# The output projection's first tile moves into attention's last steps, and two residual tiles are loaded with it

## The chip, the cores and the metric

The kernel runs on one core of one Trainium2 chip. Its time is the device time of one execution in microseconds (us), and lower is better. The profile's engines are PE (TensorE: matmuls and transposes), PEld (its weight loads), DVE (VectorE), ACT (ScalarE), POOL (GpSimd) and SP (SyncE, which issues most DMAs).

## What is computed

Two layers over 1024 frames of width 1024: one with a recurrent mixer, one with chunked attention, each with a squared-ReLU MLP behind it. The change is in the second layer, between attention's last head and the end of the output projection:

```python
def chunk_attention(hn, w_q, q_norm_g, rel_bias, w_o, k_pad, v_pad):
    ...
    out = lax.map(one_chunk, (q_chunks, jnp.arange(n_chunks)))     # 16 heads of 64
    out = out.transpose(1, 0, 2, 3, 4).reshape(bsz, s, d)
    return out @ w_o
...
h = h + g1[:, None, :] * y                                         # y: what attention returns
hn = modulate(rms_norm(h, norm2_g[layer]), sh2, sc2)
h = h + g2[:, None, :] * sqrelu_mlp(hn, mlp_w1[layer], mlp_w2[layer])
```

## The kernel before

Activations lie transposed: a tile of h, of attention's output or of a product has 128 features on the partitions and 1024 frames along the free dimension, so each is a list of 8 tiles. A product is made in halves of 512 frames, one PSUM bank each. For accuracy every operand is split into a high part and the remainder, and `mm3` makes three matmuls of each product (high by high, high by low, low by high: L329, L330, L331).

**Attention** goes in 64 steps, `todo`: 16 heads `hd`, four steps `j` each, 256 queries a step. Iteration `n` of the loop issues `scores` of step `n`, `trans` of step `n - 3` and `values` of step `n - 4`. `scores` writes a score tile of two PSUM banks (pool `ps2`, two such tiles), and DVE (L1569), ACT (L1571) and POOL (L1576) make softmax weights of it in SBUF. `trans` transposes these on PE (L1601) into up to three banks of pool `pa` (four banks), and `split` copies each to SBUF as high part (ACT, L334) and remainder (DVE, L335). `values` multiplies by V (L1620, L1621) into one more bank of `pa` for two steps together; behind an odd `j`, ACT (L1628) and DVE (L1629) read it out. Behind the last step of an odd head, POOL makes of the pair of heads the operand of the output projection, `oh[p]` (L1633) and `ol[p]` (L1635). There are eight pairs, the last behind step 63.

**The output projection** comes behind the loop. The pools of attention are closed, and a new pool `pz` takes all eight banks. The eight tiles of h are loaded back from DRAM (`hsp`) on ACT's queue (L1668). For each of eight tiles `m` of the result and each half, `proj` makes 8 x 3 = 24 matmuls, one `mm3` for each pair `k`, and DVE evicts the bank by multiplying by the gate and adding h (L1674). `n4_.sq` then stores the tile half to DRAM from SP's queue (L599) and squares it on ACT for the next norm. The last four tiles run in `tail`, with the norm between.

**Weights** come through `ws`, a stream: SP loads a tile (L159), ACT and DVE split it (L196, L200), and `ws.next()` hands it out in order: eight tiles of `w_o`, then the MLP's `w1`. Two steps before the end of attention `ws.hold` is lifted, and the stream loads and splits the first tiles of `w_o` beside the last head.

**What sets the order.** Up to L1162 the order is written by hand; from there the Tile framework's scheduler places each instruction on its engine's queue when the program is built, and within a queue each engine goes in that order. Dependencies go by tiles: the first user of a tile waits for the last user of what lay there before.

Of the kernel before, what the change touches and what calls it, by code (L numbers as in the profile page):

```python
# [8 lines left out]
F32 = mybir.dt.float32  # L9
F32R = mybir.dt.float32r  # L10
AF = mybir.ActivationFunctionType
ALU = mybir.AluOpType
# [4 lines left out]
KD = 8  # L17
# [286 lines left out]
def trunk(ctx: ExitStack, tc: tile.TileContext, I, out, dbg=None, stop=None):  # L304
    nc = tc.nc
    V, A_, PE, G = nc.vector, nc.scalar, nc.tensor, nc.gpsimd
# [6 lines left out]
    pools = {"b": pp.__enter__()}  # L313
    dp = ctx.enter_context(tc.tile_pool(name="dp", bufs=1, space=bass.MemoryType.DRAM))
    cnt = [0]

    def slot(dt=F32, tag="a", shape=(128, 1024)):
        cnt[0] += 1
        return ap_.tile(list(shape), dt, name=f"s{cnt[0]}", tag=tag)

    def bank(shape=(128, 512)):
        cnt[0] += 1
        return pools["b"].tile(list(shape), F32, name=f"b{cnt[0]}", tag="b")

    def hs(half):
        return slice(half * HALF, (half + 1) * HALF)

    def mm3(ps, ah, al, bh, bl, start, stop, more=False):
        PE.matmul(ps, ah, bh, start=start, stop=False, skip_group_check=more)  # L329
        PE.matmul(ps, ah, bl, start=False, stop=False, skip_group_check=more)  # L330
        return PE.matmul(ps, al, bh, start=False, stop=stop, skip_group_check=more).ins  # L331
# [19 lines left out]
    mods = [cp.tile([128, 48], F32, name=f"mod{l}") for l in range(2)]  # L351
    kvmod = cp.tile([128, 16], F32, name="kvmod")
    aa = cp.tile([128, 40], F32, name="aa")


    ws = Stream(nc, slot, whp, wsp)
# [291 lines left out]
    def proj(it, half, hh, hl):  # L648

        ps = bank()  # L650
        for k in range(KD):
            c = slice(k * 128, (k + 1) * 128)
            mm3(ps, it["hi"][:, c], it["lo"][:, c], hh[k][:, hs(half)], hl[k][:, hs(half)],
                k == 0, k == KD - 1)
        return ps
# [420 lines left out]
    h = []  # L1076
# [56 lines left out]
    for j in range(4):  # L1133
        for e in range(2):
            chunk(j, 1, e)
            n = 2 * j + e
# [16 lines left out]
    def mlp(l, h, nrm, nxt, last=None):  # L1153
        with ExitStack() as given:
            if l:
                given.enter_context(tc.manual_schedule())
            ws.timed = ws.early = True
            h = mlp_body(l, h, nrm, nxt, last)
            ws.drain()
            ws.timed = ws.early = False  # L1160
        if l == 0:
            order.close()  # L1162
        return h
# [210 lines left out]
    h = mlp(0, h, n2, n3)  # L1374
# [5 lines left out]
    hsp = dp.tile([KD, 128, S], F32, name="hsp")  # L1380
# [45 lines left out]
    for g in range(2):  # L1426
# [7 lines left out]
        out=gqk, in0=gqk, scalar=-(HD ** -0.5), in1=gk, op0=ALU.mult, op1=ALU.mult))  # L1434
# [40 lines left out]
    for n in range(2):  # L1475
        x1, x2, x3 = slot(F32R), slot(F32R), slot(F32R)

        def view(t):
            return t.rearrange("p (n q) -> p n q", n=4)


        hi = [view(x1)[:, 0:2], view(x1)[:, 2:4], view(x2)[:, 0:2]]
        lo = [view(x3)[:, 0:2], view(x3)[:, 2:4], view(x2)[:, 2:4]]
# [59 lines left out]
    def widths(i):  # L1543
        return 128 * min(3, max(0, i - 1))

    def scores(hd, j):
        R = prep[hd]
        bn = bns[hd % 2]
        ptile = []
        sm = cp.tile([128, 8], F32, name=f"sm{hd}_{j}", tag="sm", bufs=4)  # L1550
        for e in range(2):
            i = 2 * j + e
            w = widths(i)
            ql = R["q"][:, i * 128 : (i + 1) * 128]
            cnt[0] += 1
            sc = pools["s"].tile([128, 1024], F32, name=f"sc{cnt[0]}", tag="s")
            if w:
                k0 = (i - 1) * 128 - w
                PE.matmul(sc[:, 512 - w : 512], ql, R["k"][:, k0 : k0 + w], start=True, stop=False)
                PE.matmul(sc[:, 512 - w : 512], ql, R["kl"][:, k0 : k0 + w], start=False, stop=True)  # L1560
            c0 = 128 if i == 0 else 0
            k0 = max(0, (i - 1) * 128)
            k1 = (i + 1) * 128
            PE.matmul(sc[:, 512 + c0 : 768], ql, R["k"][:, k0:k1], start=True, stop=False)
            PE.matmul(sc[:, 512 + c0 : 768], ql, R["kl"][:, k0:k1], start=False, stop=True)
            m, s1 = sm[:, e : e + 1], sm[:, 2 + e : 3 + e]
            lo = 384 + c0 - w
            p = slot()
            V.tensor_tensor_reduce(out=p[:, lo:640], in0=sc[:, lo + 128 : 768], in1=bn[:, lo:640],  # L1569
                                   op0=ALU.add, op1=ALU.min, scale=1.0, scalar=BIG, accum_out=m)  # L1570
            A_.activation(out=p[:, lo:640], in_=p[:, lo:640], func=AF.Exp, scale=-1.0, bias=m,  # L1571
                          accum_out=s1)
            ptile.append((p, lo))
        V.reciprocal(out=sm[:, 4:6], in_=sm[:, 2:4])  # L1574
        for e, (p, lo) in enumerate(ptile):
            G.tensor_scalar(out=p[:, lo:640], in0=p[:, lo:640], scalar1=sm[:, 4 + e : 5 + e],  # L1576
                            scalar2=1.0, op0=ALU.mult, op1=ALU.mult)
        ptile = [p for p, lo in ptile]
        return ptile
# [3 lines left out]
    oh, ol = [None] * 8, [None] * 8  # L1583
# [58 lines left out]
    N = len(todo)  # L1642
    LAG = 3
    for n in range(N + LAG + 1):
        if n < N:
            hd, j = todo[n]
            if j >= 1 and hd + 1 < NH:
                prepare(hd + 1, j - 1)
            if j == 2 and hd == NH - 1:
                ws.hold = None  # L1650
                ws.pump()
            ptl[n] = scores(hd, j)
        if 0 <= n - LAG < N:
            trans(*todo[n - LAG], ptl.pop(n - LAG), n - LAG)
        if 0 <= n - LAG - 1 < N:
            values(*todo[n - LAG - 1], n - LAG - 1)
# [2 lines left out]
        return  # L1659


    ps2.__exit__(None, None, None)
    pp.__exit__(None, None, None)
    pp = ctx.enter_context(tc.tile_pool(name="pz", bufs=8, space=bass.MemoryType.PSUM))
    pools["b"] = pp
    h = [slot() for _ in range(KD)]
    for k in range(KD):
        nc.scalar.dma_start(h[k], hsp[k])  # L1668
    n4_ = NormS(h, aa[:, 24:32], mods[1][:, 24:32])
    g1b = mods[1][:, 16:24]  # L1670

    def oproj(m, it, half):
        ps = proj(it, half, oh, ol)
        V.scalar_tensor_tensor(out=h[m][:, hs(half)], in0=ps, scalar=g1b[:, m : m + 1],  # L1674
                               in1=h[m][:, hs(half)], op0=ALU.mult, op1=ALU.add)
        return [m]

    for m in range(4):
        it = ws.next()
        for half in range(2):  # L1680
            oproj(m, it, half)
            n4_.sq(m, hs(half))
        ws.done(it)
    its = [ws.next() for _ in range(4)]
    tail(its, lambda n, it, half: oproj(4 + n, it, half), n4_)
    dump("h3", h)

# [107 lines left out]
```

## Time and profile before

| | us |
|---|---|
| median of 3 runs | 2350.58 (2346.15 to 2351.51) |
| the profiled execution, its own time | 2348.78 |
| its span in the trace | 2346.9 |
| TensorE busy | 2256.5 (96% of the span) |
| VectorE busy | 1755.0 (75%) |
| ScalarE busy | 1245.0 (53%) |
| GpSimd busy | 396.1 (17%) |

All times below are from the span's start. A row of a timeline gives start, duration, engine, line, operation, tiles and count, and in brackets how long the engine had been idle before it and what released it. The granted clock (PEclk) is a share of TensorE's full 2.4 GHz.

### The profile page before, as it was taken

The numbers are of one execution on the slowest core, as the hardware profiler recorded it, in microseconds if no ns is written. First come the engines' busy times: TensorE is split into PE (matmuls) and PEld (weight loads), VectorE is DVE, ScalarE is ACT, GpSimd is POOL, SyncE is SP. The second block draws the span as 40 slices with busy tenths as digits, with TensorE's granted clock in tenths as the row PEclk, the third lists the DMA queues.
The fourth block names the chain that finished last, engine by engine and source line by source line (L and its number), as shares of the span: only waits on it lengthen the run. The fifth ranks groups of instructions, "written<-read, shape, count | busy, mean of one in ns | idle before, by whom it ended". The sixth has DMA issues, their size and how long they took to land.

```text
span 2346.9 us, 29502 instructions
## 1 busy us (share of the span) xinstructions
PE 2256.5 (96%) x10588; PEld 1872.1 (80%) x10588; DVE 1755.0 (75%) x2580; ACT 1245.0 (53%) x2148; POOL 396.1 (17%) x419
## 2 busy tenths in 40 slices
PE   4999989999999999999999989999999999899999
PEld 2877767878888778887888879997888888678887
DVE  8688887688787877777774669996496555877775
ACT  5587773375555633344443249995275555633332
POOL 0001010000000033330000068873000000033332
PEclk9999999999999999999999999999999999999999
DMA  8225466426676864545344200014114444854444
GB/s 316 72 82 145 129 200 214 179 72 241 242 255 233 316 226 157 154 162 195 101 139 143 73 12 11 12 57 146 68 50 174 166 172 176 300 209 155 150 145 142
DMA packets 141630, 363.31 MB, mean 155 GB/s; under 512 B 14924, under 2 KB 17100, under 8 KB 141484
## 3 DMA queue, kind: packets, MB, share of 16 engines
q1 hardware_dynamic: 113756, 278.45, 35.0%
q10 hardware_dynamic: 23824, 71.44, 8.1%
q0 software_dynamic: 3904, 11.54, 1.9%
q8 instruction: 83, 1.36, 0.2%
q14 instruction: 63, 0.52, 0.1%
HBM read 260.19 MB, written 89.65 MB: 149 GB/s over the span
## 4 chain that ended last, share of the span: by engine, by line
PE 69%; DVE 7%; ACT 6%; issue 4%; DMA 4%; POOL 2%; POOLq 0%; SPq 0%; ACTq 0%; DVEq 0%
PE b L331 21%; PE b L329 21%; PE b L330 21%; DMA ws<-hid 2%; PE b L1601 2%; ACT s L1571 1%; PE b L1620 1%; ACT s L334 1%; DVE wl L200 1%; PE b L1621 1%; DMA ws<-in_w_dram 1%; DVE s L200 1%; POOL ws L126 1%; DVE ws L126 1%; DMA s<-s 1%
## 5 line engine op out<-in xcount | busy, mean ns | idle before, releaser
L329 PE MATMUL b<-s,wh 128*128 128x512 f32 (+1 forms) x2532 | 997.5, 394 | 22.4 <-DVE s L1286 9.1
L330 PE MATMUL b<-s,wh 128*128 128x512 f32 (+1 forms) x2532 | 993.4, 392 | 18.7 <-DVE s L200 9.7
L331 PE MATMUL b<-s,wl 128*128 128x512 f32 x2296 | 901.2, 393 | 6.9 <-DVE wl L200 6.9
L329 PEld LDWEIGHTS b<-s,wh 128*128 128x128 f32 (+1 forms) x2532 | 477.4, 189 | 133.7 <-ACT wh L196 10.4
L330 PEld LDWEIGHTS b<-s,wh 128*128 128x128 f32 (+1 forms) x2532 | 477.5, 189 | 125.7 <-DVE s L200 11.3
L196 ACT ACTIVATE wh<-ws 128x1024 fp32r<-128x1024 f32 (+3 forms) x302 | 291.4, 975 | 484.1 <-POOL ws L126 265.4
L331 PEld LDWEIGHTS b<-s,wl 128*128 128x128 f32 x2296 | 432.9, 189 | 102.6 <-DVE wl L200 9.6
L200 DVE TENSOR_TENSOR wl<-ws,wh 128x1024 fp32r<-128x1024 f32 (+1 forms) x249 | 304.1, 1223 | 109.2 <-ACT wh L196 105.3
L1286 DVE SCALAR_TENSOR_TENSOR s<-b,mod,s 128x512 f32<-128x512 f32 x221 | 164.6, 745 | 91.8 <-PE b L331 91.2
L200 DVE TENSOR_TENSOR s<-ws,s 128x512 fp32r<-128x512 f32 x284 | 224.3, 804 | 4.9 <-ACT s L196 4.9
L126 POOL TENSOR_TENSOR ws<-ws 128x512 f32<-128x512 f32 x21 | 27.5, 1310 | 1107.1 <-DVE s L1286 449.7
L196 ACT ACTIVATE s<-ws 128x512 fp32r<-128x512 f32 x284 | 164.9, 618 | 70.0 <-DMA ws<-hid 35.8
L330 PE MATMUL b<-wl,s 128*128 128x512 f32 x384 | 149.9, 390 | 0.0
L329 PE MATMUL b<-wh,s 128*128 128x512 f32 x384 | 148.9, 389 | 0.0
L331 PE MATMUL b<-wh,s 128*128 128x512 f32 x384 | 146.4, 389 | 1.1 <-DVE s L584 1.1
L1264 DVE TENSOR_TENSOR s<-s,b 128x512 f32<-128x512 f32 x84 | 57.4, 683 | 113.7 <-PE b L331 102.7
L1262 ACT ACTIVATE s<-b 128x512 f32<-128x512 f32 x84 | 50.1, 596 | 101.7 <-PE b L331 101.0
L362 DVE CUSTOM_DVE_ANT_0 ws<-ws,cb,vec 128x1024 f32<-128x1024 f32 x59 | 75.1, 1280 | 33.9 <-DMA ws<-in_ada_dram 27.0
L331 PE MATMUL b<-s,wh 128*128 128x512 f32 x236 | 91.8, 389 | 0.0
L335 DVE TENSOR_TENSOR s<-b,s 128x384 fp32r<-128x384 f32 x144 | 82.6, 592 | 12.2 <-ACT s L334 11.8
L1576 POOL TENSOR_SCALAR s<-s,sm 128x640 f32<-128x640 f32 (+4 forms) x128 | 86.1, 685 | 22.0 <-DVE sm L1574 20.4
L1571 ACT ACTIVATE s<-s,sm 128x640 f32<-128x640 f32 (+4 forms) x128 | 88.3, 696 | 1.6 <-DVE sm L1569 1.6
(165 smaller groups left out, 2985.2 us busy)
## 6 DMA issues: line engine op xcount, KB each, us to landing
hid<-s ACTq DMA_DIRECT2D x128, 512.0 KB, 4.9
ws<-hid SPq DMA_DIRECT2D x118, 512.0 KB, 4.5
ws<-in_w_dram SPq DMA_DIRECT2D x220, 256.0 KB, 3.5
ws<-in_ada_dram SPq DMA_DIRECT2D x56, 512.0 KB, 4.6
s<-in_ada_dram SPq DMA_DIRECT2D x40, 512.0 KB, 9.0
ws<-in_w_in_dram SPq DMA_DIRECT2D x22, 512.0 KB, 7.8
hsp<-s SPq DMA_DIRECT2D x32, 256.0 KB, 2.0
s<-hsp SPq DMA_DIRECT2D x16, 512.0 KB, 7.4
```

The lines of the kernel that those rows point to most:

```text
L126: eng.tensor_tensor(out=out, in0=in0, in1=in1, op=op)
L196: self.nc.scalar.activation(out=hi[:rows, :n], in_=src, func=AF.Copy)
L200: self.nc.vector.tensor_tensor(out=lo[:rows, :n], in0=src, in1=hi[:rows, :n].bitcast(F32), op=ALU.subtract)
L329: PE.matmul(ps, ah, bh, start=start, stop=False, skip_group_check=more)
L330: PE.matmul(ps, ah, bl, start=False, stop=False, skip_group_check=more)
L331: return PE.matmul(ps, al, bh, start=False, stop=stop, skip_group_check=more).ins
L335: V.tensor_tensor(out=lo, in0=src, in1=hi.bitcast(F32), op=ALU.subtract)
L362: V.tensor_tensor_reduce(out=t, in0=t, in1=cb, op0=ALU.mult, op1=ALU.add, scale=1.0, scalar=bias, accum_out=dst)
L1264: V.tensor_tensor(out=t, in0=t, in1=ps, op=ALU.add)
L1286: V.scalar_tensor_tensor(out=t, in0=ps, scalar=g2[:, m : m + 1], in1=t, op0=ALU.mult, op1=ALU.add)
L1571: A_.activation(out=p[:, lo:640], in_=p[:, lo:640], func=AF.Exp, scale=-1.0, bias=m, accum_out=s1)
L1576: G.tensor_scalar(out=p[:, lo:640], in0=p[:, lo:640], scalar1=sm[:, 4 + e : 5 + e], scalar2=1.0, op0=ALU.mult, op1=ALU.mult)
```

## The change

At the loop's iteration 64, after the last `scores` and ahead of `trans` of step 61 in the code, the first projection tile is begun. It takes one score tile of pool `ps2`, named `po`, whose two banks hold its two halves, and the first weight tile from the stream. For both halves it makes the products of pairs 0 to 6, 2 x 7 x 3 = 42 matmuls. The eighth pair's six matmuls follow behind the loop, still ahead of the closing of attention's pools, with both evictions (`oadd`, which is the eviction of before under a name of its own). The remaining seven tiles are made as before. Tiles 0 and 1 of h are loaded on SP's queue with the early products (L1657); the other six stay on ACT's (L1677).

```diff
+        if n == N:
+
+            h = [slot() for _ in range(2)]
+            for k in range(2):
+                nc.sync.dma_start(h[k], hsp[k])
+            wo0 = ws.next()
+            cnt[0] += 1
+            po = pools["s"].tile([128, 1024], F32, name=f"po{cnt[0]}", tag="s")
+            for half in range(2):
+                for k in range(KD - 1):
+                    c = slice(k * 128, (k + 1) * 128)
+                    mm3(po[:, hs(half)], wo0["hi"][:, c], wo0["lo"][:, c], oh[k][:, hs(half)],
+                        ol[k][:, hs(half)], k == 0, False, True)
         if 0 <= n - LAG < N:
             trans(*todo[n - LAG], ptl.pop(n - LAG), n - LAG)
...
+    h += [slot() for _ in range(2, KD)]
+    for k in range(2, KD):
+        nc.scalar.dma_start(h[k], hsp[k])
+    n4_ = NormS(h, aa[:, 24:32], mods[1][:, 24:32])
+    g1b = mods[1][:, 16:24]
+
+    def oadd(m, half, ps):
+        V.scalar_tensor_tensor(out=h[m][:, hs(half)], in0=ps, scalar=g1b[:, m : m + 1],
+                               in1=h[m][:, hs(half)], op0=ALU.mult, op1=ALU.add)
+
+    for half in range(2):
+        c = slice((KD - 1) * 128, KD * 128)
+        mm3(po[:, hs(half)], wo0["hi"][:, c], wo0["lo"][:, c], oh[-1][:, hs(half)],
+            ol[-1][:, hs(half)], False, True, True)
+        oadd(0, half, po[:, hs(half)])
+        n4_.sq(0, hs(half))
+    ws.done(wo0)
     ps2.__exit__(None, None, None)
...
-    h = [slot() for _ in range(KD)]
-    for k in range(KD):
-        nc.scalar.dma_start(h[k], hsp[k])
...
     def oproj(m, it, half):
-        ps = proj(it, half, oh, ol)
-        V.scalar_tensor_tensor(out=h[m][:, hs(half)], in0=ps, scalar=g1b[:, m : m + 1],
-                               in1=h[m][:, hs(half)], op0=ALU.mult, op1=ALU.add)
+        oadd(m, half, proj(it, half, oh, ol))
         return [m]

-    for m in range(4):
+    for m in range(1, 4):
```

The order of each engine's instructions is the scheduler's. On PE, behind the transposes of step 61 (reading `s_13698`), before: `b` are banks of `pa`, `s_10408` and `s_10410` the split weights of step 61, `v_13599` the last head's V, `s_13779` and `s_13787` step 62's weights; the brackets name the engines whose semaphores a row waits for.

```order
L1601 MATMUL b_13866<-ident,s_13698 128x128 [waits Pool_49]
L1601 MATMUL b_13866<-ident,s_13690 128x128
L1601 MATMUL b_13866<-ident,s_13698 128x128
L1601 MATMUL b_13873<-ident,s_13698 128x128 x2
L1620 MATMUL b_13879<-s_10408,v_13599 128x256 [waits Activation_49]
L1601 MATMUL b_13884<-ident,s_13779 128x128 [waits DVE_49,Pool_49]
L1601 MATMUL b_13884<-ident,s_13779 128x128
L1601 MATMUL b_13884<-ident,s_13787 128x128 [waits Pool_49]
```

The same place in the changed kernel, where `s_11012` and `s_11013` are the first pair's high part and remainder and `wh_13749`, `wl_13750` those of the first weight tile:

```order
L1601 MATMUL b_13913<-ident,s_13698 128x128 [waits Pool_49]
L1601 MATMUL b_13913<-ident,s_13690 128x128
L1601 MATMUL b_13913<-ident,s_13698 128x128
L1601 MATMUL b_13920<-ident,s_13698 128x128 x2
L329 MATMUL po_13870<-s_11012,wh_13749 128x512 [waits DVE_49]
L330 MATMUL po_13870<-s_11013,wh_13749 128x512
L331 MATMUL po_13870<-s_11012,wl_13750 128x512
```

All 42 early products stand together between the transposes of step 61 and the next instruction of attention; the transposes of step 62 and the value products of step 61 follow them, and behind those the rest in the order of before.

On PE at the first products of the eighth pair (`s_13961`, `s_13962`), before; `b_13988` and `b_14017` are the first tile's two halves, and `s_13646`, `s_13647` the seventh pair:

```order
L329 MATMUL b_13988<-s_13646,wh_13749 128x512
L330 MATMUL b_13988<-s_13647,wh_13749 128x512
L331 MATMUL b_13988<-s_13646,wl_13750 128x512
L329 MATMUL b_14017<-s_11012,wh_13749 128x512
L330 MATMUL b_14017<-s_11013,wh_13749 128x512
L329 MATMUL b_13988<-s_13961,wh_13749 128x512 [waits Pool_49]
L331 MATMUL b_14017<-s_11012,wl_13750 128x512
L329 MATMUL b_14017<-s_11451,wh_13749 128x512
```

The same products in the changed kernel, where the eighth pair is `s_14008`, `s_14009`, and `b_14050` the second tile's first half:

```order
L1620 MATMUL b_13980<-s_10409,v_13599 128x256
L1621 MATMUL b_13980<-s_10409,v_13599 128x256
L329 MATMUL po_13870<-s_14008,wh_13749 128x512 [waits Pool_49]
L330 MATMUL po_13870<-s_14009,wh_13749 128x512 [waits Pool_49]
L331 MATMUL po_13870<-s_14008,wl_13750 128x512
L329 MATMUL po_13870<-s_14008,wh_13749 128x512 [waits DVE_49]
L330 MATMUL po_13870<-s_14009,wh_13749 128x512
L331 MATMUL po_13870<-s_14008,wl_13750 128x512
L329 MATMUL b_14050<-s_11012,wh_13755 128x512 [waits DVE_49,Activation_49]
```

The eighth pair's six products now follow the last value products directly. By the counts in the program, the first wait for DVE is for the eviction of `po`'s first half, and the second, ahead of the second tile, for that of its second half. On DVE and POOL nothing else changes place.

## Rows read from the trace of the kernel before

**Rows 1.** From the page: the chain that ended last, by engine.
```profile
PE 69%; DVE 7%; ACT 6%; issue 4%; DMA 4%; POOL 2%; POOLq 0%; SPq 0%; ACTq 0%; DVEq 0%
```

**Rows 2.** Waits, 1604 to 1630, then PE's to 1760: total us, times, longest.
```profile
PE b L1620 <- ACT s L334: 2.5, 1, 2.5
...
PE b L329 <- DVE s L1629: 2.0, 1, 2.0
PE b L550 <- DVE s L542: 0.4, 1, 0.4
```

**Rows 3.** Timeline of PE, 1604 to 1619.
```profile
1604.62 0.71 PE L1601 MATMUL b<-ident,s 128*128 128x128 f32 x5
1607.88 0.58 PE L1620 MATMUL b<-s,v 128*128 128x256 f32 x1 [2.55 <-ACT s L334]
...
1611.48 1.58 PE L1601 MATMUL b<-ident,s 128*128 128x128 f32 x10
1613.26 0.39 PE L1620 MATMUL b<-s,v 128*128 128x256 f32 x1 [0.20 <-DVE s L1629]
...
1618.43 0.50 PE L329 MATMUL b<-s,wh 128*128 128x512 f32 x1 [2.03 <-DVE s L1629]
```

**Rows 4.** Timelines of ACT, DVE and POOL, 1595 to 1636.
```profile
1611.89 0.59 ACT L1628 ACTIVATE s<-b 64x512 f32<-64x512 f32 x1
...
1603.29 0.82 DVE L1569 CUSTOM_DVE_ANT_0 s<-sc,s 128x640 f32<-128x640 f32 x1
...
1616.43 1.22 DVE L200 TENSOR_TENSOR wl<-ws,wh 128x1024 fp32r<-128x1024 f32 x1 [1.58 <-PE b L1621]
...
1629.64 0.75 DVE L1674 SCALAR_TENSOR_TENSOR s<-b,mod,s 128x512 f32<-128x512 f32 x1 [1.97 <-PE b L331]
...
1635.09 0.75 DVE L1674 SCALAR_TENSOR_TENSOR s<-b,mod,s 128x512 f32<-128x512 f32 x1 [3.35 <-PE b L331]
...
1595.55 2.40 POOL L1635 TENSOR_TENSOR s<-s,s 128x1024 fp32r<-128x1024 f32 x1
...
1618.53 1.06 POOL L1633 TENSOR_SCALAR s<-s 128x1024 fp32r<-128x1024 f32 x1 [7.58 <-DVE s L1629]
1619.67 2.40 POOL L1635 TENSOR_TENSOR s<-s,s 128x1024 fp32r<-128x1024 f32 x1
```

**Rows 5.** Busy time by stretch; behind POOL the granted clock, DMA share, GB/s.
```profile
478.31:480.90 2.59, 2.59 (x6) 2.11 (x7) 2.59 (x4) 0.00 (x0) 0.00 (x0) 0.50 0.01 3
...
799.27:805.20 5.93, 5.93 (x14) 4.67 (x15) 5.93 (x10) 5.46 (x11) 0.00 (x0) 0.50 1.05 387
...
1607.60:1610.90 3.30, 3.02 (x14) 3.02 (x15) 2.42 (x6) 2.51 (x6) 1.88 (x3) 0.50 0.71 235
1611.10:1613.00 1.90, 1.79 (x15) 1.38 (x13) 1.25 (x3) 1.57 (x4) 0.00 (x0) 1.00 0.00 0
1616.40:1618.43 2.03, 0.00 (x1) 0.00 (x1) 1.91 (x2) 0.59 (x1) 0.00 (x0) 1.00 0.47 143
...
2045.66:2051.20 5.54, 5.54 (x13) 4.43 (x14) 3.81 (x6) 2.27 (x4) 0.00 (x0) 0.50 1.00 325
...
350.70:358.00 7.30, 6.54 (x15) 4.66 (x16) 5.12 (x7) 0.00 (x0) 0.71 (x2) 0.50 1.04 332
```

**Rows 6.** Timeline of PE from 478, products after an idle time.
```profile
478.31 0.80 PE L330 MATMUL b<-s,wh 128*128 128x512 f32 x1 [3.44 <-DVE s L623]
478.90 0.63 PE L331 MATMUL b<-s,wl 128*128 128x512 f32 x1
479.33 0.63 PE L329 MATMUL b<-s,wh 128*128 128x512 f32 x1
```

**Rows 7.** Timelines: DMA issues of SP and ACT, and ACT's first split of w1.
```profile
1605.33 12.72 SPq L159 DMA_DIRECT2D ws<-in_w_dram  x3
...
1616.44 8.58 ACTq L1668 DMA_DIRECT2D s<-hsp  x8
...
1689.32 1.06 ACT L196 ACTIVATE wh<-ws 128x1024 fp32r<-128x1024 f32 x1 [3.86 <-PE b L330]
```

More of the change, by code (lines that the diff above doesn't have):

```diff
@@ L1665, in trunk @@
     pools["b"] = pp
-    h = [slot() for _ in range(KD)]
-    for k in range(KD):
-        nc.scalar.dma_start(h[k], hsp[k])
-    n4_ = NormS(h, aa[:, 24:32], mods[1][:, 24:32])
-    g1b = mods[1][:, 16:24]
     def oproj(m, it, half):
-        ps = proj(it, half, oh, ol)
-        V.scalar_tensor_tensor(out=h[m][:, hs(half)], in0=ps, scalar=g1b[:, m : m + 1],
-                               in1=h[m][:, hs(half)], op0=ALU.mult, op1=ALU.add)
+        oadd(m, half, proj(it, half, oh, ol))
         return [m]
-    for m in range(4):
+    for m in range(1, 4):
         it = ws.next()
```

## The prediction

> **What bounds the kernel now.** I read the page's chain first, then the PE waits around the end of attention, then the timelines of the engines there, and last the granted clock by stretch. TensorE makes 69% of the chain that ended last [rows 1]. So a change of order pays only where PE stands idle or runs at its low clock. Around the change there are two such places: 2.5 us before L1620, released by ACT's L334, and 2.0 us before the first output product L329, released by DVE's L1629 [rows 2]. From there until 1760 us PE waits 0.4 us once [rows 2], so a delay at the start of the output projection is passed on one for one.
>
> To follow the sum, call the last attention steps 61, 62 and 63 (head 15, j = 1, 2, 3), T their transposes (L1601) and V their value products (L1620, L1621). Before: T61 ends at 1605.33, PE idles to 1607.88, T62 and V61 follow, then T63, then V62 and V63 from 1613.26 to about 1616.4, then idle to 1618.43, where the projection begins [rows 3]. From 1607.6 to 1610.9 the granted clock is 0.50 (1.2 GHz of 2.4), after that idle time; from 1611.1 on it is 1.00 [rows 5]. The 2.0 us of idle time at 1616.4 is not followed by a drop: the record stays at 1.00 through it [rows 5].
>
> **The change part by part.**
>
> *The 42 early products.* They are the same instructions, moved, not added. One costs (1635.09 - 1629.64) / 24 = 0.227 us, from two neighbouring evictions of 24 products each [rows 4]. The block is 42 x 0.227 = 9.5 us, and PE takes instructions in order, so T62 now starts at 1605.3 + 9.5 = 1614.8. Its inputs are there: POOL finished the seventh pair at 1595.55 + 2.40 = 1597.95 [rows 4], and DVE's L1569 has read the score tile whose banks it takes, the one wait that the order shows on it, at 1603.29 + 0.82 = 1604.1 [rows 4]. What it hides: ACT's and DVE's work on T61's tiles, which PE waited for.
>
> *The steps behind it.* T62 (10) and V61 (8) at 0.12 us each, the rate of the ten transposes of 1.58 us less their tail [rows 3], end at 1614.8 + 18 x 0.12 + 0.2 = 1617.15. T63 runs while V61 is read out. V62 has to wait for V61's bank: from L1628's start to PE's restart took 1613.26 - 1611.89 = 1.37 us before [rows 3, 4], so it starts at 1618.5. V62 and V63 took 1613.26 to 1616.4 [rows 3, 4], 3.15 us, and end at 1621.65. That is 5.25 us later than before for 9.5 us of work taken in: 4.3 us are won, which is the 2.5 us of idle time plus half of the 3.3 us at 0.50, and a little.
>
> *The handover.* Here cover is lost. After V63 come L200 and L1629 on DVE, then L1633 and L1635 on POOL, which make the eighth pair: L200 starts at 1616.43, L1635 ends at 1619.67 + 2.40 = 1622.07 [rows 4]. That is 5.65 us. Before, PE worked from 1618.43 on with the seven pairs that it had, since the products of the eighth were put far behind. Now those 42 are gone, and the rows of the order show the products of the eighth pair next on PE, in order, with a wait for POOL on each new operand. So the first low product L330 can start at 1621.65 + 5.65 + 0.1 = 1627.4. In between PE has one product, L329.
>
> *Two evictions that PE now waits for.* In the new order the second half's L329 waits for DVE, and so does the first product of the next tile. By the count on each wait these are the first and the second eviction of `po`. An eviction is 0.75 us [rows 4], with 0.1 for both handovers. What is queued behind each is all of the projection.
>
> *The clock there.* No row of before has PE at this place idle from 1621.65 to 1627.4 but for one product. Idle times of 2.5 us here and of 3.4 us ahead of 478.31 ended at 0.50 [rows 3, 5, 6]; the one of 2.0 us did not. I take 0.50. At that clock products start 0.43 apart and one lasts 0.63; the first lasts 0.8 and the next starts 0.59 after it [rows 6]. Half 0: 0.59 + 0.63, to 1628.6. Eviction to 1629.45. Half 1: 0.59 + 0.43 + 0.63, to 1631.1. Eviction, and the next tile starts at 1631.95. Before, the same product began at 1629.64 - 0.16 = 1629.5 (0.39 us of the product before, less 0.23). This makes +2.5. At full clock each half would end some 0.6 us sooner, and it would be +1.3.
>
> *After the restart.* The low clock stays a while. It lasted 2.6 us and a bit from 478.31 on, 3.1 from 1607.88, 5.5 from 2045.66, 5.9 from 799.27 and 7.3 from 350.70 [rows 5]. Each us costs 1 - 0.227 / 0.43 = 0.47. The ends are 1.3 (2.8 us) and 2.9 (6.2 us), with 350.70 apart, since PE was idle again within it. I take 4.4 us, the mean of the four others: 2.1.
>
> *Sum:* +2.5 + 2.1 = +4.6 us, between 3.8 and 5.4.
>
> *The loads.* Two of h's tiles move from ACT's queue to SP's, ahead of three weight loads. Those were issued from 1605.33 over 12.7 us; the first of them is split at 1689.32 at the earliest, which is some 70 us of cover [rows 7]. If that cover were gone, every us of lateness would be a us. The other six now start about 5.3 us later, with the end of attention, where eight began at 1616.44 [rows 7]; they were issued over 8.6 us, so the six are out by about 1628. The first is needed by the third tile's first eviction, three half tiles after 1631.95, at 1648. I cost both at nothing. The first `h` tile did not hold the projection before either, as its first evictions were released by PE.
>
> *What the order asks and what the banks ask.* The row of the order has `po`'s second half waiting for an eviction of its first. The Trainium skill, "PSUM — Partial Sum Buffer", section on bank collisions, says that a bank is a memory of its own and that a matmul may write one while another engine reads a different one. By that rule both evictions could run beside PE's work, and the sum would be that of the third rival, +2.4, instead of +4.6. The wait is in the program whatever the banks could do, so I keep it.
>
> **The rivals.**
>
> 1. *The low clock stays long.* Mechanism: PE's short bursts between the evictions don't bring the clock back, as in 350.70 to 358.0, where 7.3 us passed at 0.50 with idle time within [rows 5]. Place: the products from 1627.4 on. Price: 7.3 x 0.47 = 3.4 behind the restart, so 2.5 + 3.4 = +5.9, 2356.5 us. It decides from 4.7 us on (2.5 + 0.47 x 4.7 = 4.7 us, the bound of "slower"). For it: PE's work comes in pieces here too. Against: in four of five rows it was over sooner, in two of them under 4.7 us and in two over, which is why the forecast itself lies on the line.
> 2. *The clock stays up.* The one product in the gap, or where the gap falls, keeps it, as at 1616.4. Then +1.3, 2351.9 us. Against: the gap is 5.7 us with one product in it, and the longest that passed in these rows 2.0.
> 3. *The two waits for evictions cost nothing.* Half 0's last product starts at 1627.4 + 0.59 = 1628.0; three more follow at 0.43, and the next tile starts at 1629.7 in place of 1631.95 [rows 6]. That is +2.4, 2353.0 us. Against: both waits stand in the order.
> 4. *The block fills idle time and opens none.* That is, the eighth pair would be there when PE asks. Gain: 2.5 + 2.0 of idle time and 0.5 x 3.3 of low clock, 6.2 us, 2344.4 us. Against: L1633 and L1635 still come behind V63, 3.5 us from start to end [rows 4], and PE has nothing else ahead of the wait.
> 5. *The block doesn't run where it stands,* since its bank or the h load holds it. A late start is paid one for one from 1605.3 on; 1 us gives 2356.2 us. Against: the score tile was read 1.2 us before T61's end [rows 3, 4].
>
> **How the numbers follow.** The profiled execution's own time is 2348.78 us, its span 2346.9; the median of the runs shown is 2350.58, which is 1.8 us above it. I put the difference of +4.6 on the median: 2355.2 us (in a profiled execution 2353.4). The bound of what a measurement of this kernel can tell from no change, 0.2%, is 4.7 us, so the forecast sits on it: I can say that nothing is won, not on which side of that line it falls. Chances: forecast 0.62 (own range 2354.4 to 2356.0; half of it under the line, half over), rival 1 0.13, rival 2 0.10, rival 3 0.05, rival 4 0.05, rival 5 0.02. The last 0.03 is for low-clock stretches elsewhere, in the last layer's MLP, that fall otherwise when all is moved by some us: the 5.5 us at 2045.66 [rows 5] are worth 2.6 us either way. Faster: rival 4 and some of the last, 0.07. Within 0.2%: half the forecast, rivals 2 and 3 and some of the last, 0.47. Slower: the rest, 0.46. The range leaves out rival 4 and the farthest of the last two: from rival 2 less 1.4 for the spread of the runs, 2350.5, to rival 1 with 2 us of it, 2358.5.
>
> **What would show it.** In the changed kernel's timeline: 42 products in a row for 9.5 us with no idle time ahead; L1620's wait for L334 gone; V63 ending 5.25 us later against T61's end; then PE waiting for POOL's L1633 and L1635 some 3 and 2 us, then twice for the eviction, with the second tile's first product 26.6 us after T61's end, 24.2 before. The granted clock should be 0.50 from within the gap to some 4.5 us after the restart. I am wrong if PE's wait for POOL is short (then the handover is mis-sized), if the clock stays at 1.00 (rival 2), or if a weight or an h tile is waited for later in the projection.

## The result, and the profile after

The changed kernel took **2352.43 us** (median of 22 runs, 2349.32 to 2358.32), the kernel before 2348.03 us in the same sessions (22 runs, 2343.86 to 2351.51). The ratio is 1.002, with a 95% interval of 1.0014 to 1.0027: 4.4 us slower, between 3.3 and 6.3. The forecast was +4.6 us. The kernel before came out 2.5 us lower with 22 runs than with the three that the prediction had, so the difference is what is compared here, not the 2355.2 us.

The chain that ended last is still mostly TensorE's (69% before [rows 1]):

```profile
PE 78%; DVE 8%; ACT 6%; DMA 3%; issue 3%; POOL 1%; SPq 0%; DVEq 0%; ACTq 0%; POOLq 0%
```

The waits of PE from 1600 to 1640 us, in the changed kernel (total us, times, longest):

```profile
PE po L329 <- POOL s L1633: 3.2, 1, 3.2
PE po L330 <- POOL s L1635: 1.6, 1, 1.6
PE b L329 <- DVE s L1682: 0.9, 1, 0.9
PE po L329 <- DVE s L1682: 0.8, 1, 0.8
...
```

Against [rows 2]: L1620's 2.5 us for ACT's L334 are gone, and so are the 2.0 us for L1629 ahead of the first output product. In their place stand four waits, 6.65 us in all by the rows below: two for the eighth pair, which POOL makes, and two for evictions of `po`. The timeline of PE shows where (start, duration, engine, line, operation, count, idle time before and who ended it):

```profile
1606.20 0.71 PE L1601 MATMUL b<-ident,s 128*128 128x128 f32 x5
1606.67 0.48 PE L329 MATMUL po<-s,wh 128*128 128x512 f32 x1
...
1616.08 0.39 PE L331 MATMUL po<-s,wl 128*128 128x512 f32 x1
1616.31 1.25 PE L1601 MATMUL b<-ident,s 128*128 128x128 f32 x10
...
1622.77 0.28 PE L1621 MATMUL b<-s,v 128*128 128x256 f32 x1
1626.29 0.80 PE L329 MATMUL po<-s,wh 128*128 128x512 f32 x1 [3.24 <-POOL s L1633]
1628.71 0.80 PE L330 MATMUL po<-s,wh 128*128 128x512 f32 x1 [1.63 <-POOL s L1635]
...
1630.78 0.80 PE L329 MATMUL po<-s,wh 128*128 128x512 f32 x1 [0.84 <-DVE s L1682]
...
1633.36 0.77 PE L329 MATMUL b<-s,wh 128*128 128x512 f32 x1 [0.94 <-DVE s L1682]
```

Read it from the top. Step 61's transposes end at 1606.91. The 42 early products follow without a gap, and step 62's transposes behind them; the last value product ends at 1623.05. Then PE has one product in 5.66 us. What it waits for is on POOL:

```profile
1625.19 1.04 POOL L1633 TENSOR_SCALAR s<-s 128x1024 fp32r<-128x1024 f32 x1 [12.64 <-DVE s L1629]
1626.32 2.34 POOL L1635 TENSOR_TENSOR s<-s,s 128x1024 fp32r<-128x1024 f32 x1
```

The same two instructions, just as long, stood behind the value products before [rows 4]. There PE, after 2.0 us of idle time, worked beside them on products of the first seven pairs. The clock (granted clock third from the end of a row, 1.00 is 2.4 GHz, 0.50 is 1.2 GHz), by stretches of the changed kernel:

```profile
1622.00:1624.00 2.00, 1.05 (x9) 0.85 (x8) 0.91 (x1) 0.59 (x1) 0.00 (x0) 1.00 0.00 0
1624.00:1626.00 2.00, 0.00 (x0) 0.00 (x0) 1.00 (x2) 0.00 (x0) 0.81 (x1) 0.81 0.86 313
1626.00:1628.00 2.00, 0.80 (x1) 0.29 (x1) 0.00 (x0) 0.00 (x0) 1.92 (x2) 0.50 0.98 373
...
1633.00:1638.00 5.00, 4.64 (x11) 3.70 (x12) 1.35 (x2) 0.72 (x2) 0.00 (x0) 0.50 0.80 281
1638.00:1639.00 1.00, 1.00 (x4) 0.77 (x4) 0.00 (x0) 0.00 (x0) 0.00 (x0) 0.55 0.03 12
1639.00:1641.00 2.00, 2.00 (x10) 1.65 (x9) 0.00 (x0) 0.00 (x0) 0.00 (x0) 1.00 0.00 0
```

It falls in the gap, stays at 0.50 through the eighth pair's products, and for some 5.5 us more after the second tile has begun.

**A measure for what follows.** "The stretch" is the time from the end of step 61's transposes to the start of the second tile's second eviction. Before, that eviction is this row of DVE's timeline, and the stretch is 1640.53 - 1605.33 = 35.20 us (the start from [rows 3]):

```profile
1640.53 0.75 DVE L1674 SCALAR_TENSOR_TENSOR s<-b,mod,s 128x512 f32<-128x512 f32 x1 [3.25 <-PE b L331]
```

In the changed kernel it is 1647.15 - 1606.91 = 40.24 us:

```profile
1647.15 0.75 DVE L1682 SCALAR_TENSOR_TENSOR s<-b,mod,s 128x512 f32<-128x512 f32 x1 [3.24 <-PE b L331]
```

That is 5.0 us more. At the last eviction of the projection it is still 5.0 us (107.36 us after step 61's transposes, and 102.31 before). The kernel before and the changed one:

```profile
1707.64 0.75 DVE L1674 SCALAR_TENSOR_TENSOR s<-b,mod,s 128x512 f32<-128x512 f32 x1
```
```profile
1714.27 0.75 DVE L1682 SCALAR_TENSOR_TENSOR s<-b,mod,s 128x512 f32<-128x512 f32 x1
```

But the two profiled spans differ by 2.0 us only (2346.9 and 2348.9), although the changed kernel's profile was 1.6 us late already at the end of step 61's transposes, where nothing is changed. So 4.6 us were won back later, in the last layer's MLP (634.6 us from the projection's last eviction to the end of the span, and 639.2 before). Before, PE waited 2.68 us for L200 there and ran at 0.50 behind it; in the changed kernel it waited 1.48 us, and the clock stayed up. The kernel before, its PE timeline and a stretch behind it:

```profile
2070.33 0.50 PE L331 MATMUL b<-s,wl 128*128 128x512 f32 x1 [2.68 <-DVE wl L200]
```
```profile
2072.00:2074.00 2.00, 2.00 (x7) 1.52 (x6) 1.47 (x4) 0.00 (x0) 0.00 (x0) 0.50 0.93 314
```

The changed kernel, the same:

```profile
2074.45 0.50 PE L331 MATMUL b<-s,wl 128*128 128x512 f32 x1 [1.48 <-DVE wl L200]
```
```profile
2076.50:2078.50 2.00, 2.00 (x11) 1.65 (x10) 2.00 (x4) 0.94 (x2) 0.00 (x0) 1.00 1.05 267
```

Further profiles of the same two kernels (below) show that this is not the change's doing. So one span against one span says little at this size. The stretch and the medians are what the experiments go by.

### The profile page after: what moved, and what is told of

It is laid out like the page before. It is cut to its first block, busy times and chain, and to the rows that moved or that the text cites. A ratio compares the mean times of both kernels' runs of the same rounds, so it can differ in the third digit from the quotient of the medians.

```text
span 2348.9 us, 29506 instructions
## 1 busy us (share of the span) xinstructions
PE 2258.4 (96%) x10588; PEld 1873.4 (80%) x10588; DVE 1755.9 (75%) x2580; ACT 1245.5 (53%) x2148; POOL 396.2 (17%) x419
## 4 chain that ended last, share of the span: by engine, by line
PE 78%; DVE 8%; ACT 6%; DMA 3%; issue 3%; POOL 1%; SPq 0%; DVEq 0%; ACTq 0%; POOLq 0%
PE b L331 24%; PE b L329 24%; PE b L330 24%; PE b L1601 1%; DMA hid<-s 1%; ACT s L1571 1%; DVE wl L200 1%; PE b L1620 1%; DVE s L200 1%; ACT s L334 1%; DMA ws<-hid 1%; PE b L1621 1%; DMA ws<-in_w_dram 1%; DVE s L1182 1%; DVE ws L126 1%
## 5 line engine op out<-in xcount | busy, mean ns | idle before, releaser
L329 PE MATMUL b<-s,wh 128*128 128x512 f32 (+1 forms) x2516 | 992.3, 394 | 19.3 <-DVE s L1286 7.7
L330 PE MATMUL b<-s,wh 128*128 128x512 f32 (+1 forms) x2516 | 988.5, 393 | 16.9 <-DVE s L200 8.0
L329 PEld LDWEIGHTS b<-s,wh 128*128 128x128 f32 (+1 forms) x2516 | 475.0, 189 | 129.2 <-ACT wh L196 7.4
L330 PEld LDWEIGHTS b<-s,wh 128*128 128x128 f32 (+1 forms) x2516 | 475.2, 189 | 123.8 <-DVE s L200 9.6
L196 ACT ACTIVATE wh<-ws 128x1024 fp32r<-128x1024 f32 (+3 forms) x302 | 291.4, 975 | 478.0 <-POOL ws L126 266.6
L200 DVE TENSOR_TENSOR wl<-ws,wh 128x1024 fp32r<-128x1024 f32 (+1 forms) x249 | 303.8, 1222 | 94.9 <-ACT wh L196 91.2
L200 DVE TENSOR_TENSOR s<-ws,s 128x512 fp32r<-128x512 f32 x284 | 222.9, 800 | 6.0 <-ACT s L196 6.0
L196 ACT ACTIVATE s<-ws 128x512 fp32r<-128x512 f32 x284 | 165.2, 618 | 77.1 <-DMA ws<-hid 42.7
L330 PE MATMUL b<-wl,s 128*128 128x512 f32 x384 | 149.9, 390 | 0.0
L329 PE MATMUL b<-wh,s 128*128 128x512 f32 x384 | 149.0, 389 | 0.0
```

Of the source, the lines that this page charges most:

```text
L196: self.nc.scalar.activation(out=hi[:rows, :n], in_=src, func=AF.Copy)
L200: self.nc.vector.tensor_tensor(out=lo[:rows, :n], in0=src, in1=hi[:rows, :n].bitcast(F32), op=ALU.subtract)
```

## The experiments

**Theory.** The early block itself is a gain, but it takes from the handover the work that hid the making of the eighth pair. The loss is that gap, the low clock behind it, and two waits for evictions. **Rivals:** the block's place costs something of its own; the loads on SP do; the waits for evictions, or for the eighth pair, cost nothing since something else ends last; the clock falls whatever PE does.

### Cover for the handover

```
...
+    wo1 = ws.next()
+    p1 = [bank() for _ in range(2)]
+    for half in range(2):
+        for k in range(KD - 1):
+            ck = slice(k * 128, (k + 1) * 128)
+            mm3(p1[half], wo1["hi"][:, ck], wo1["lo"][:, ck], oh[k][:, hs(half)],
+                ol[k][:, hs(half)], k == 0, False, True)
+    for half in range(2):
+        last(wo0, po[:, hs(half)], half)
+    for half in range(2):
         oadd(0, half, po[:, hs(half)])
         n4_.sq(0, hs(half))
     ws.done(wo0)
+    for half in range(2):
+        last(wo1, p1[half], half)
+        oadd(1, half, p1[half])
+        n4_.sq(1, hs(half))
...
-    for m in range(1, 4):
+    for m in range(2, 4):
```

> The changed kernel with one thing more: the second output tile's 42 products of the seven early pairs stand behind the last attention step and ahead of the eighth pair's products, in two ordinary banks, so that PE has 9.5 us of work while DVE and POOL make the eighth pair (5.65 us). Theory (the handover lost its cover): PE has no wait of over 0.3 us for POOL's L1633 or L1635, the granted clock stays at 1.00 from the last value products on, and from the end of step 61's transposes to the second tile's second eviction it is about 29 us, where the kernel before took 35.2 and the changed one 40.2. Time: some 10.5 us less than the changed kernel, 6 less than before, ratio to before 0.9974 (0.997 to 0.998). Rival 1 (the early block itself costs, through its place in attention, and not what it leaves uncovered): the time stays within 1.5 us of the changed kernel's, ratio 1.001 to 1.0025. Rival 2 (the idle time moves: PE waits elsewhere in the projection for weights or h tiles instead): ratio 0.999 to 1.001, with a new wait in the projection of several us.

Measured: 2344.0 us against 2349.0 of the kernel before, ratio 0.9979 (0.997 to 0.9989), by the ratio 4.9 us faster. The stretch is about 29.6 us (the second of a pair of evictions in one row). PE's waits from 1600 to 1765:

```profile
PE b L329 <- ACT s L538: 2.0, 1, 2.0
PE b L550 <- DVE s L542: 0.4, 1, 0.4
PE b L1620 <- DVE s L1629: 0.3, 1, 0.3
```

No wait for POOL is left, although the eighth pair is no sooner done: 5.67 us behind the last value product (1631.44 - 1625.77). The scheduler put eleven of the 42 products among the last value products and the rest behind them. The stretches of this kernel around it:

```profile
1616.00:1625.80 9.80, 9.54 (x67) 8.60 (x67) 4.00 (x7) 3.37 (x7) 0.00 (x0) 1.00 0.00 1
1625.80:1631.40 5.60, 5.60 (x26) 4.60 (x26) 1.91 (x2) 0.60 (x1) 3.40 (x2) 1.00 0.74 265
...
1638.00:1641.20 3.20, 3.20 (x9) 2.45 (x8) 2.87 (x4) 0.60 (x2) 0.00 (x0) 0.50 0.91 305
```

In the second row POOL is busy for 3.40 us and PE for all 5.60, at full clock. The stretch is 10.2 us shorter than the changed kernel's mean (39.81, below). Not all of that is cover: the edit also puts both evictions of the first tile behind the eighth pair's products of both halves (`last` makes those of one half), so the changed kernel's waits of 0.84 and 0.94 us for evictions go from this place too. That leaves some 8 us for the cover and the clock with it. The early block stands exactly where the change put it, so its place does not explain the loss; the lost cover does. The gain is some 1 us short of the 6 expected, within the interval, and the trace shows a loss that the theory did not have (rival 2 in part): a new wait of 2.0 us ahead of the third tile, with 3.2 us at 0.50 behind it. The row names ACT's L538, but by the program PE waits there for the last of four evictions, which ended at 1637.41, 0.14 us before PE went on:

```profile
1636.01 1.40 DVE L1682 SCALAR_TENSOR_TENSOR s<-b,mod,s 128x512 f32<-128x512 f32 x2
```

All four come at once now, since the eighth pair's products of both tiles do, and the third tile's bank lies in a pool that opens only when attention's banks are free.

### No wait between the halves

```
-            po = pools["s"].tile([128, 1024], F32, name=f"po{cnt[0]}", tag="s")
+            po = [pools["s"].tile([128, 1024], F32, name=f"po{cnt[0]}_{e}", tag="s") for e in range(2)]
...
```

> The changed kernel with the two halves of the first output tile in two score tiles in place of one, so that the second half's products do not wait for the eviction of the first half. Theory (the order's wait costs what it shows, 0.75 us of eviction and 0.1 of handovers, and the next tile's wait stays): PE's wait for DVE between the halves is gone, 0.8 to 1.0 us less than the changed kernel, ratio to before about 1.0015. Rival (the waits for the evictions cost nothing, because POOL's second result is what ends last): within 0.3 us of the changed kernel, ratio 1.002.

Measured: 2351.76 us, ratio 1.0009 (1.0 to 1.0018), by the ratio 2.1 us slower than before. The stretch is 38.93 us. The waits, 1600 to 1765:

```profile
PE po L329 <- POOL s L1633: 3.2, 1, 3.2
PE po L330 <- POOL s L1635: 1.7, 1, 1.7
PE b L329 <- DVE s L1682: 0.9, 1, 0.9
...
```

The 0.8 us between the halves are gone, nothing takes their place, and the stretch is shorter than that of the changed kernel in each of three profiles (40.24, 39.58 and 39.61, below), by 0.9 us of their mean. So the wait costs about what the row says; this version has one profile, and against the nearest of the three the gain is 0.65. The two intervals of the times overlap, so the trace decides here.

### PE kept busy in the gap

```
+    pd = pools["s"].tile([128, 1024], F32, name="pd", tag="s")
+    late = ws.items[wo0["n"] + 3]["lo"][:, 0:128]
+    for _ in range(20):
+        PE.matmul(pd[:, :HALF], late, oh[0][:, :HALF], start=True, stop=True)
```

> The changed kernel with 20 extra products of 128x512 on PE, whose result nobody reads, in the gap behind the last value products: they start when DVE's L200 is done (1.3 us after the last value product) and last 4.5 us, to about the end of POOL's L1635. The wait for the eighth pair stays as long as it was, only PE is not idle in it. Theory (some 3.3 us of the loss are the clock: 0.8 at the slow start of the eighth pair's six products and 2.5 in the 5.3 us of low clock behind them): the granted clock is 1.00 from the last value products on, and the time 2.5 to 3.5 us under that of the changed kernel, ratio to before 1.0005 to 1.001. Rival (the clock falls whatever PE does there, or its price is small): low clock as before, time within 0.5 us of the changed kernel's or over it by up to 0.5 us, ratio 1.002.

Measured: 2348.11 us, ratio 0.9997 (0.9987 to 1.0006). The stretch is 36.92 us, 2.9 less than the changed kernel's mean. PE's timeline, the extra products and the eighth pair's first:

```profile
1623.64 4.83 PE L1688 MATMUL pd<-s,wl 128*128 128x512 f32 x20 [1.32 <-DVE wl L200]
1628.31 0.39 PE L329 MATMUL po<-s,wh 128*128 128x512 f32 x1
```

And the clock, from the gap into the second tile:

```profile
1624.00:1629.00 5.00, 5.00 (x23) 3.92 (x21) 0.30 (x1) 0.00 (x0) 3.45 (x2) 1.00 1.01 365
1629.00:1633.00 4.00, 2.22 (x9) 1.44 (x9) 2.65 (x3) 2.29 (x3) 0.00 (x0) 1.00 1.01 393
1633.00:1638.00 5.00, 5.00 (x24) 4.12 (x23) 0.42 (x2) 0.00 (x0) 0.00 (x0) 1.00 0.70 241
```

The eighth pair is no earlier, and both waits for evictions are still there (0.84 and 0.93 us; the profile puts the second down to ACT's L196, which ended 0.07 us behind the eviction). Only the clock is other, and that alone gives 2.9 us back of the 4.0 that the change costs in the stretch (below). The 1.1 us left are what the new waits cost beyond what the early block wins. By the time this version is 0.7 us under the kernel before, lower than the expected 1.0005 to 1.001; the interval still reaches into that range, and the size is taken from the stretch.

### A shorter making of the eighth pair

```
+                if p == 7:
+                    A_.activation(out=oh[p], in_=opair[p], func=AF.Copy)
+                    V.tensor_tensor(out=ol[p], in0=opair[p], in1=oh[p].bitcast(F32),
+                                    op=ALU.subtract)
+                else:
...
```

> The changed kernel, where the eighth pair's two parts are made by ACT (the high one) and DVE (the remainder) and no longer by POOL; the other seven pairs as they were. Theory (each us of the eighth pair's making is a us of the end): 128x1024 takes ACT 1.06 us, where POOL takes 1.05, and DVE 1.2 us for the remainder, where POOL takes 2.35. PE's second wait falls from 1.6 to some 0.5 us; 1.0 to 1.4 us less than the changed kernel, ratio to before 1.0013. If the gap becomes short enough for the clock to stay up, up to 4 us less, ratio 1.0002. Rival (PE's wait is not for the eighth pair's values, but for the loads or the evictions behind): within 0.3 us of the changed kernel, ratio 1.002.

Measured: 2351.26 us, ratio 1.0009 (0.9999 to 1.002). The stretch is 38.23 us, 1.6 less than the changed kernel's mean; the clock fell here too, to 0.50 for some 10 us. The waits:

```profile
PE po L329 <- ACT s L1634: 3.1, 1, 3.1
...
PE po L330 <- DVE s L1635: 0.5, 1, 0.5
```

The second wait falls from 1.6 to 0.5 us: DVE takes 1.23 us for what takes POOL 2.34. PE does wait for the eighth pair, and the time that its making is shorter comes back. The time alone could not tell this from the rival.

### The loads alone

```
+        if n == N:
+            h = [slot() for _ in range(2)]
+            for k in range(2):
+                nc.sync.dma_start(h[k], hsp[k])
...
```

This is put into the kernel before, with the products where they were.

> The kernel before with the loads alone: the first two of h's tiles are issued by SP at the point where the changed kernel issues them, and ACT issues the other six at the end of attention. The products stay where they were. Theory (the loads cost and bring nothing): within 1 us of the kernel before, ratio 0.9997 to 1.0005, PE's waits at the handover 2.5 and 2.0 us as before. Rival (part of the changed kernel's loss comes from the loads, which delay the weights behind them on SP): 1 to 4 us slower than before, ratio 1.0005 to 1.0017, with a wait for a weight in or behind the projection.

Measured: 2348.91 us against 2348.71, ratio 0.9999 (0.999 to 1.0009), with the waits of 2.5 and 2.0 us as before and no new one behind. The loads cost nothing that the time can tell (2.3 us either way), and no wait shows a cost. But the stretch is 36.74 us, 1.5 more than in the first profile of the kernel before, and the clock says why: behind L1629's 2.0 us the kernel before stayed at 1.00 [rows 5], and this one did not:

```profile
1618.50:1619.00 0.50, 0.50 (x3) 0.42 (x4) 0.00 (x0) 0.00 (x0) 0.47 (x1) 1.00 0.99 385
1619.00:1622.50 3.50, 3.50 (x10) 2.74 (x9) 0.00 (x0) 0.00 (x0) 2.94 (x2) 0.51 1.00 371
```

### The two kernels once more

Was that the loads, or does the fall come and go? Two more profiles of each kernel, unchanged, tell.

> The kernel before, unchanged, for a second profile. In the run with the loads alone, whose handover is the same, the clock fell to 0.50 behind the 2.0 us of idle time, for 3.6 us; in the first profile of the kernel before it stayed at 1.00. Theory (the fall behind so short an idle time comes and goes from one execution to the next): it may stay or fall; from the end of step 61's transposes to the second tile's second eviction 35.2 us where it stays, 36.7 where it falls. Rival (the loads made it fall, through the memory traffic or the shift of some us): 1.00 again, 35.2 within 0.2.

> The kernel before, unchanged, for a third profile; theory and rival as for the second: 35.2 us or 36.7 by the one, 35.2 within 0.2 by the other.

> The changed kernel, unchanged, for a second profile. Theory: at its longer gap (3.24 and 1.63 us of idle time) the clock falls each time, only the end of the low stretch moves, so that the same stretch takes 39.5 to 41 us. Rival (here too the fall comes and goes): 37 us where the clock stays up, as in the run with the extra products.

> The changed kernel, unchanged, for a third profile; theory and rival as for the second: 39.5 to 41 us by the one, 37 in some profiles by the other.

The kernel before: 36.54 and 35.57 us. Its second profile, behind the waits of 2.55 and of 2.03 us:

```profile
1609.50:1612.50 3.00, 3.00 (x16) 3.00 (x15) 1.87 (x5) 1.87 (x5) 1.57 (x2) 0.50 0.44 156
...
1619.90:1623.00 3.10, 3.10 (x9) 2.42 (x8) 0.00 (x0) 0.00 (x0) 2.37 (x1) 0.50 0.91 350
```

Its third, at the same two places:

```profile
1612.00:1615.00 3.00, 2.54 (x20) 2.30 (x20) 2.75 (x6) 2.73 (x7) 1.58 (x3) 1.00 0.68 254
...
1622.00:1625.00 3.00, 3.00 (x8) 2.33 (x8) 0.00 (x0) 0.00 (x0) 2.92 (x2) 0.50 0.84 317
```

The same two idle times gave "low, full" in the first profile, "low, low" in the second, "full, low" in the third. So it was not the loads: the clock behind an idle time of 2.0 or 2.55 us comes and goes. My numbers had only the first and second of these outcomes in them, 35.2 and 36.7; 35.57 is a third.

The changed kernel took 39.58 and 39.61 us, at 0.50 from the gap until about 4 us into the second tile both times. The second profile of it:

```profile
1623.00:1632.00 9.00, 5.97 (x12) 3.84 (x13) 2.64 (x3) 2.32 (x3) 1.20 (x1) 0.50 0.99 355
1632.00:1633.00 1.00, 1.00 (x4) 0.79 (x3) 0.00 (x0) 0.00 (x0) 0.00 (x0) 0.51 0.84 342
```

Three profiles of each give means of 35.77 and 39.81 us: the change costs 4.0 us in the stretch, beside 4.4 us (3.3 to 6.3) in the time. Behind the projection nothing is lost or won on the mean: from its last eviction to the end of the span the three profiles of the kernel before took 639.2, 637.2 and 636.4 us, those of the changed one 634.6, 639.2 and 639.0, with a mean of 637.6 for either kernel. As whole runs the two new ones of the changed kernel are no slower (2350.2 and 2349.9 us against 2348.7 and 2351.0), since they came to the end of step 61's transposes 3 to 8 us sooner, in work that is the same in both kernels. The changed kernel was not timed again beside the experiments; against the kernel before, the stretch puts the first four of them (in the order above: cover, two tiles, extra products, shorter making) at -6.2, +3.2, +1.2 and +2.5 us, each inside the interval of its time.

### All banks in turn

The covered version, with its new wait mended: the score tiles' pool alone is closed, and its four banks are used by turns with attention's four. One thing more is changed, in lines not shown here: of the second tile's early products the last nine (three pairs of its second half) now stand behind the eighth pair's products of the first tile. Which of the two takes the wait away is not tested apart.

```
...
     ps2.__exit__(None, None, None)
-    pp.__exit__(None, None, None)
-    pp = ctx.enter_context(tc.tile_pool(name="pz", bufs=8, space=bass.MemoryType.PSUM))
-    pools["b"] = pp
+    ctx.push(pp)
+    both = [pools["b"], ctx.enter_context(tc.tile_pool(name="pz", bufs=4, space=bass.MemoryType.PSUM))]
+
+    class Both:
+        n = 0
+
+        def tile(self, *a, **kw):
+            self.n += 1
+            return both[self.n % 2].tile(*a, **kw)
+
+    pools["b"] = Both()
```

> The version with the covered handover (second tile's products behind the last attention step), mended where its trace showed a new wait: there the four evictions of the two first tiles came at once, and PE waited 2.0 us for the last of them, and ran 3.3 us at the low clock behind it, since the third tile's bank is in a pool that opens only when all of attention's banks are free. Here attention's four ordinary banks stay in use, the four of the score tiles come back beside them, and the two sets are used by turns; so the third tile waits for no eviction of the second. Theory (idle time and the clock behind it are all that is to be had): no wait over 0.5 us and a granted clock of 1.00 from the end of step 61's transposes to the third tile's last eviction, which takes 6.64 us of attention and 144 products of 0.227 us, 39.5 us in all, where the kernel before took 46.1, the changed one 51.1 and the first covered version 43.3. Time: 6 to 6.6 us less than before, ratio 0.9972 to 0.9975. Rival (the gain is given back later, since the projection's end is set by weights, norms or the MLP behind it): as the first covered version, ratio 0.9979 or nearer to 1, with a new wait later in the stage.

Measured: 2343.44 us against 2348.71, ratio 0.998 (0.997 to 0.999). The first four tiles went as the theory had it, with no wait and at full clock. From the end of step 61's transposes to the fourth tile's last eviction:

```profile
1604.40:1654.60 50.20, 49.95 (x245) 42.01 (x245) 21.26 (x32) 14.83 (x27) 7.56 (x6) 1.00 0.44 152
```

PE is busy for 49.95 of 50.20 us at full clock, while DVE evicts bank after bank beside it. The waits for evictions in the changed kernel came from the program. The Trainium skill, "PSUM — Partial Sum Buffer", section on bank collisions, says that a matmul may write one bank while another engine reads a different one. This trace agrees with the page. The fourth tile's last eviction comes at 50.2 us, which is 6.64 us of attention and 192 products of 0.227 us. (The third tile's comes at 41.2 and not at 39.5, since some of the fourth tile's products went ahead of it.) Before, the fourth tile's last eviction came 56.96 us after step 61's transposes, 6.7 us later:

```profile
1662.29 0.75 DVE L1674 SCALAR_TENSOR_TENSOR s<-b,mod,s 128x512 f32<-128x512 f32 x1 [3.19 <-PE b L331]
```

At the projection's last eviction the lead is only 4.5 us (97.78 against 102.31), and the waits to 1765 say where the rest went:

```profile
PE b L330 <- DVE s L623: 1.5, 1, 1.5
PE b L550 <- DVE s L542: 1.3, 1, 1.3
```
```profile
1700.00:1704.00 4.00, 2.47 (x11) 1.91 (x11) 4.00 (x6) 4.00 (x8) 0.00 (x0) 1.00 0.44 152
```

At the end of the projection DVE and ACT are busy throughout, with the norm of the first half, the last evictions and the splits of the next weights, and PE waits for them. So both were right in part: the idle time was to be had, but some 2 us of it are given back where DVE and ACT become the bound. This version is not measurably faster than the first covered one; both are 0.2% faster than the kernel before.

## Why the prediction was right

- **The early block** (9.5 us forecast): 1616.31 - 1606.91 = 9.4 us, with no idle time ahead. Right, as was the bank that it takes. Rival 5 falls.
- **The steps behind it** (V63 ends 5.25 us later): 16.14 us after T61's end, 11.07 before, so 5.07. Right. This is the part in which the change wins.
- **The handover** (5.65 us from V63's end to L1635's, 0.1 more to L330): 1628.71 - 1623.05 = 5.66. Right, and rival 4 falls. That lost cover is the cause is shown by the first experiment, where some 8 of the 10.2 us that come back in the stretch are not waits for evictions.
- **Two evictions** (0.85 each): 0.84 and 0.94. Right; one was taken out alone and gave 0.9 against the mean. Rival 3 falls with it. Its reason, that banks could be written and read side by side, is borne out by the version with all banks in turn and did not apply to this program.
- **The second tile's start** (26.6 us after T61's end): 1633.36 - 1606.91 = 26.45.
- **The low clock** (0.50 from within the gap, 4.4 us after the restart): 5.5 us in the first profile, 4.1 and 4.2 in the two others, mean 4.6. Rival 2 (stays up) falls, and so does rival 1 (7.3 us), though the first profile lies over the 4.7 us from which it would have decided. That the clock costs this much is shown by the extra products: 2.9 us, where the prediction's own terms give 1.2 (2.5 less 1.3) + 2.1 = 3.3.
- **The loads** (nothing): 0.9999, and no wait for a weight or an h tile in the projection.
- **What was mis-sized** is the base. The prediction took from [rows 5] that the 2.0 us of idle time before L329 leave the clock at 1.00, and set the second tile's start against that. In the three other profiles with this handover the clock fell behind it, and in one of them it stayed up behind the 2.55 us. On the mean the kernel before is 0.6 us worse off than I had it (35.77 for 35.20), so the cost is nearer to 4.0 us than to 4.6 or to the 5.0 between the first profile of each. It is the first term that shrinks: on the mean the second tile starts 1.8 us later, not 2.5, and what comes behind that start adds 2.3, where 2.1 was put. The difference is within the interval of the times, so that these came out 0.2 us from the forecast is in part luck.
- **The time itself.** 2352.43 us lies 2.8 under the forecast's 2355.2 and outside its own range, 2354.4 to 2356.0; it is nearer to the times of rivals 2 and 3 (2351.9 and 2353.0). All but 0.2 us of that is the median of before, which three runs put 2.55 us too high. It is the rows and not the time that tell the forecast from these rivals.
- **The 0.2% line.** The forecast lay on it, and so does the result, 1.0014 to 1.0027. The last MLP, with its reserve of 2.6 us either way, moves single profiles by up to 4.6 us, but the means of three are the same in both kernels.

## What to carry to other kernels

Before work is moved forward to fill an idle time, look at what it hides where it stands: here 9.5 us of products filled 2.5 us of waiting and left PE with one product in 5.7 us, of which 2.0 us had been idle before too, at a place where nothing else was ready, and low clock came on top. Fill the first gap, and put the next ready work into the place that became empty; the block and its replacement together gain 0.2%, where the block alone costs 0.2%. Give it banks that the next tile does not wait for, and look for the engine that is late next: here the norm at the projection's end.

## What the hardware showed

- The same idle time of PE, 2.0 us long, was followed by the low clock in three of four profiles of this handover, and one of 2.55 us in three of four as well, in no fixed combination. The gap of 1.3 us in the run with the extra products left the clock up, those of 3.2 and 1.6 us in the changed kernel brought it down in three of three profiles.
- 20 products whose result nobody reads, put into a wait of 5.7 us, shortened what follows by 2.9 us, though nothing that PE waited for came earlier.
- The low clock that a gap left behind around this handover lasted 3.1 to 6.2 us after PE had steady work again. Elsewhere in the kernel before, some 2.6 us from 478.31 and 7.3 us from 350.70, where PE was idle again within it [rows 5].
